# Spreading the later keys of a gated DeltaNet layer over more merge gates, and loading and pausing the triangular solve differently

## The chip, the core and the metric

The kernel runs on one core of a Trainium2 chip. The metric is device time in microseconds (us) of one execution. The engines are TensorE (PE, matmuls and transposes), VectorE (DVE), ScalarE (ACT), GpSimd (POOL) and SyncE (SP, which here issues every DMA). A difference of about 0.5% is what a measurement of this kernel can tell from no change.

## The reference, cut to what matters

One decoder layer on 512 tokens of width 2048, all in float32. After an adaptive norm, `h` is projected into many parts; a sliding-window attention and a gated DeltaNet run side by side, each goes through an output projection, and two sigmoid gates merge them.

```
proj = h @ w_in
aq, ak, av, ag, d_qkv, dz, db, da, mg_a, mg_b = jnp.split(proj, _split_points(), axis=-1)
...
d_qkv = causal_conv_silu(d_qkv, conv_w)
dq, dk, dv = jnp.split(d_qkv, [DN_KEY, 2 * DN_KEY], axis=-1)
...
L = jnp.where(strict, jnp.einsum('bhncd,bhnsd->bhncs', k_beta, k) * decay, 0.0)
t_inv = lax.linalg.triangular_solve(eye + L, jnp.broadcast_to(eye, L.shape),
                                    left_side=True, lower=True, unit_diagonal=True)
u = t_inv @ v_beta
w = t_inv @ (k_beta * jnp.exp(g)[..., None])
...
y = jax.nn.sigmoid(mg_a) * y_a + jax.nn.sigmoid(mg_b) * y_b
return x + gate * (y @ w_out)
```

There are 16 key heads and 32 value heads of width 128; `k` is normed per token, and `L` belongs to a chunk of 64 tokens. So the keys come first, then their chunk matrices `L`, then the inverse of `eye + L`, and only then can the heads (queries, values, scan) run. The merge gates `mg_a` and `mg_b` need only `h`.

## The kernel before

**Tiles.** Every projection is cut into channel tiles of 128 output channels by 512 tokens (`channel_tile`). A weight in float32 is split into a high and a low part (`split`: `whi` by ACT, `wlo` by DVE, two halves of 128x1024 each per tile), and each product is three matmuls (`mm3`, lines 237 to 239), so a tile is 48 matmuls of 128x512. After every two of its 16 steps `pump` is called: 8 pumps to a tile. All other work is written as generators that `pump` advances: `live` ones count pumps (a `yield 3` resumes three pumps later), `slow` ones get a budget per pump.

**Stages.** The start computes `h` and, in passing, the accumulators of four keys (`NST`). Then comes the stage of the keys (about 138 to 545 us of the profile): 31 tiles, namely 16 merge gates `mb`, the 12 keys 4 to 15, and 3 merge gates `ma`. The merge gates are there as PE work that asks little of others: a tanh by ACT and a store. Then 16 groups of heads of 5 tiles each, the output projections, the attention, and the end.

**A key** (`keys`, lines 648 to 692) takes about 19 pumps after its tile: convolution (ACT, then 3 DVE instructions and a silu), transposes by PE into the PSUM tile `ptk`, sums of squares by ACT (`sumsq`, four `junk`), three pumps later the norm by DVE (`rsqrt`, lines 55 to 65, and L658: a chain of eleven instructions on 128x4 elements, `ss`, `rky`, `rkt`), the scaling of `k` by ACT (L664), transposes back by PE into `ptkT` (L271), a product `pkk` by PE (L677) times the decay mask `E` (two tiles of 128x512 per key, loaded by DMA, masked by POOL in lines 710 and 711, exponentiated by ACT, multiplied by DVE in line 683), and stores of `lt_d`. `ptk`, `ptkT` and `pkk` take turns in two PSUM buffers of the tag `tp`; `E` has four buffers.

**The solve** (`solve`) inverts 64x64 triangles, 128 at once, by 124 DVE instructions (lines 754 and 761, `atmp` and `A`) for half 0 (heads 0 to 15, `s0`), and again for half 1 (`s1`). It is `slow` work: `s0` has a budget of 0.85 per pump, 1.2 from a late gate on; `s1` 0 until `s0` is done, then 1.1, and 0.6 among the heads. `solve_load` waits until the eight keys of its half have stored, loads `A` in two DMAs per 64 partitions, and lets `solve` start. `hold` is a number of pumps in which `slow` work is not advanced; in the stage of the keys (`keep_order` is true there) it has no effect.

**Order.** `mixed` sets the order of the tiles, and `plan` the order of the weight loads that follows from it: four `mb` ahead (`NFIRST`), keys 4 to 7 one after the other, then key and gate by turns (k8, mb4, k9, mb5, ... k15, mb11), then mb12 to mb15 and ma0 to ma2. The order on each engine is then set by a scheduler, which moves an instruction ahead where its buffers allow it; so DMAs and work for a later head can stand among those of an earlier one.

Of the kernel before, what the change touches and what calls it, by code (L numbers as in the profile page):

```python
# [19 lines left out]
KT = D // P  # L20
NTB = T // P
EPS = 1e-6
KH = 16
VH = 32
QH = 32
HD = 64
# [3 lines left out]
TWO_PI_LO = 3.0199159819567e-07  # L30
MAGIC = float(0x5F3759DF)
NST = 4
NFIRST = 4
STW = 320 + NST * P


class Layer:
# [43 lines left out]
    def pump(self):  # L81
        self.weight_tick()
        with self.behind() if self.keep_order else nullcontext():
            for e in list(self.live):
                e[1] -= 1
                if e[1] <= 0:
                    self.step(e)
        held, self.hold = self.hold > 0 and not self.keep_order, max(self.hold - 1, 0)
        with self.behind():
            for e in [] if held else list(self.slow):  # L90
                e[2] += e[1]
                while e in self.slow and e[2] >= e[3]:
                    e[2] -= e[3]
                    self.step_slow(e)
        for q in list(self.side.values()):
            if not q:
                continue
            q[0][2] += q[0][1]
            while q and q[0][2] >= 1.0:
                q[0][2] -= 1.0  # L100
                if next(q[0][0], True):
                    q.pop(0)
# [44 lines left out]

    def mixed(self):

        first = [("k", g) for g in range(NST, 8)]  # L150
        turns = [x for g in range(8, KH) for x in (("k", g), ("mb", g - 8 + NFIRST))]
        return first + turns + [("mb", j) for j in range(8 + NFIRST, KT)]


    def plan(self):
        a, jobs = self.a, []
        wi = lambda name, t: jobs.append((name, a["w_ch"][t]))
        jobs += [(f"st{u}", a["w_st"][u]) for u in range(KT // 2)]
        for j in range(NFIRST):
            wi(f"mb{j}", 96 + j)  # L160
# [408 lines left out]
    def conv(self, pool, ps, t, y):  # L569

        nc = self.nc
        w = self.convh[:, t, :]
        nc.scalar.activation(y, ps, AF.Copy, scale=w[:, 3:4])
        yield 1
        self.hold = max(self.hold, 1)
        for j, s in ((2, 1), (1, 2), (0, 3)):
            nc.vector.scalar_tensor_tensor(  # L577
                out=y[:, s:], in0=ps[:, : T - s], scalar=w[:, j : j + 1], in1=y[:, s:], op0=ALU.mult, op1=ALU.add
            )
        yield 2  # L580
        th = pool.tile([P, T], F32, tag="th", name="th")
        nc.scalar.activation(th, y, AF.Tanh)
        yield 1
        nc.vector.scalar_tensor_tensor(out=y, in0=th, scalar=1.0, in1=y, op0=ALU.add, op1=ALU.mult)


    def deltanet(self):
        tc, nc, a = self.tc, self.nc, self.a
        dram = self.dram
        self.lt_d = dram.tile([2, 2, 16, 4, HD, HD], F32, name="lt_d")  # L590
        self.lab_d = dram.tile([VH, HD, 4, HD], F32, name="lab_d")
        self.ta_d = dram.tile([2, 16, 4, HD, HD], F32, name="ta_d")
        self.ts_d = dram.tile([2, 2, 16, 4, HD, HD], F32, name="ts_d")
        self.kT_d = dram.tile([KH, P, T], F32, name="kT_d")
        self.k_d = dram.tile([KH, P, T], F32, name="k_d")
        self.o_d = dram.tile([VH, P, T], F32, name="o_d")
        with ExitStack() as ps:
            self.pmm = ps.enter_context(tc.tile_pool(name="pmm", bufs=2, space=PSUM, reuse_waits="tile"))
            self.ptp = ps.enter_context(tc.tile_pool(name="ptp", bufs=2, space=PSUM, reuse_waits="tile"))
            self.gwk = ps.enter_context(tc.tile_pool(name="gwk", bufs=1, reuse_waits="tile"))  # L600
            sol1 = ps.enter_context(tc.tile_pool(name="sol1", bufs=1, side="right", reuse_waits="tile"))
            with ExitStack() as sa:
                wk = sa.enter_context(tc.tile_pool(name="dnA", bufs=2, reuse_waits="tile"))
                sol0 = sa.enter_context(tc.tile_pool(name="sol0", bufs=1, reuse_waits="tile"))
                gp = sa.enter_context(tc.tile_pool(name="gates", bufs=1, reuse_waits="tile"))
                self.go(self.gates(gp), 1)
                self.keys_done, self.solve_in = [], {}
                self.keep_order = True
                for g in range(NST):
                    self.go(self.keys(wk, g, self.acc_k[g]), 10 + 8 * g)  # L610
                for j in range(NFIRST):
                    self.merge_gate("mb", j, self.mb_d)
                self.go(self.solve_load(sol0, 0), 1)
                self.go(self.solve_load(sol1, 1), 1)
                s0 = self.paced(self.solve(sol0, 0, nc.vector), 0.85)
                s1 = self.paced(self.solve(sol1, 1, nc.vector), 0.0)
                for kind, j in self.mixed():
                    if kind == "k":
                        self.go(self.keys(wk, j, self.channel_tile(f"k{j}")), 0)
                    else:  # L620
                        self.merge_gate("mb", j, self.mb_d)
                        if j == KT - 4:
                            s0[1] = 1.2
                for j in range(3):
                    self.merge_gate("ma", j, self.ma_d)
                    if s0 not in self.slow:
                        s1[1] = 1.1
                self.drain_live()
                self.drain_slow(s0)
                self.keep_order = False  # L630
                s1[1] = 0.6
            with ExitStack() as sb:
                wk = sb.enter_context(tc.tile_pool(name="dnB", bufs=2, reuse_waits="tile"))
                self.tt = []
                for n in range(4):
                    t = wk.tile([P, NTB, P], F32, tag=f"tt{n}", name=f"tt{n}", bufs=1)
                    nc.gpsimd.memset(t[HD:P, :, 0:HD], 0.0)
                    self.tt.append(t)
                for g in range(KH):
                    if g == 8:  # L640
                        self.drain_slow(s1)
                    self.heads(wk, g)
                for j in range(3, 5):
                    self.merge_gate("ma", j, self.ma_d)
                self.drain_live()
        self.dump("o", self.o_d)

    def keys(self, wk, g, ps):

        nc = self.nc  # L650
# [4 lines left out]
        self.transpose4(pt, lambda c: y[:, c * P : (c + 1) * P])  # L655
        ss = self.sumsq(wk, pt)
        yield 3
        nc.vector.tensor_scalar(out=ss, in0=ss, scalar1=EPS, scalar2=None, op0=ALU.add)  # L658
        rk = self.rsqrt(wk, ss, NTB, "rk")
        E = [self.decay_load(wk, 2 * g + e) for e in range(2)]  # L660
        yield 2
        k = wk.tile([P, NTB, P], F32, tag="k", name="k")
# [22 lines left out]
        for e in range(2):  # L685
            h = 2 * g + e
            b, hl = h // 16, h % 16
            for k2 in range(2):
                s = slice(k2 * HD, (k2 + 1) * HD)
# [24 lines left out]

    def solve_load(self, wk, b):
        nc = self.nc
        while not all(g in self.keys_done for g in range(8 * b, 8 * b + 8)):
            yield 1
        yield 3
        A = wk.tile([P, HD, HD], F32, tag=f"A{b}", name="A", bufs=1)  # L720
        bet = wk.tile([P, HD], F32, tag=f"bet{b}", name="bet", bufs=1)
        for k2 in range(2):
            s = slice(k2 * HD, (k2 + 1) * HD)
            nc.sync.dma_start(
                out=bet[s],
                in_=self.b_rows.rearrange("h (c k i) -> k (h c) i", c=4, k=2)[k2, b * HD : (b + 1) * HD, :],
            )
        for q in range(2):
            for k2 in range(2):
                s = slice(k2 * HD, (k2 + 1) * HD)  # L730
                r = slice(q * 32, (q + 1) * 32)
                nc.sync.dma_start(out=A[s, r], in_=self.lt_d[b, k2].rearrange("h c j i -> (h c) j i")[:, r])
            yield 4
        self.solve_in[b] = A, bet

    def solve(self, wk, b, eng):
# [828 lines left out]
```

## Time and profile before

| | us |
|---|---|
| median of 3 runs | 2956.26 (2944.69 to 2958.72) |
| the profiled execution | 2954.11 |
| its span | 2952.3 |
| PE busy in the span | 2879.0 (98%) |
| DVE busy in the span | 1794.3 (61%) |

Rows of groups and of the timeline name line, engine, operation and `out<-in` tile; a bracket at a row's end is the engine's idle time before it and what ended it. Rows of waits give the total, the number of times and the longest. Rows of windows give the stretch, its length, the busy time of PE, of PE's weight loads, of DVE, ACT and POOL with their instructions in brackets, the granted clock of PE as a share of full speed, the share of DMA, and GB/s. "Issue" of a DMA is on SP.

### The profile page before, as it was taken

What the parts mean: (1) busy time and instruction counts of PE and PEld (TensorE: products, weight loads), DVE (VectorE), ACT (ScalarE), POOL (GpSimd) and SP (SyncE); (2) the same over time, 40 slices, a digit from 0 to 9 for tenths busy, and PEclk for the clock granted to TensorE, in tenths of its full rate; (3) what the DMA queues carried; (4) which work ended last, traced back from release to release, by engine and by line L of the source; (5) the groups of instructions that cost most, each with busy time, mean ns of one, the idle gap of its engine ahead of it and who ended that gap; (6) DMA issues with size and microseconds to landing.
All of it is one profiled execution on the core that took longest, in us unless ns stands there. A gap on an engine that the chain in (4) does not pass through costs nothing.

```text
span 2952.3 us, 38088 instructions
## 1 busy us (share of the span) xinstructions
PE 2879.0 (98%) x14556; PEld 2358.8 (80%) x14556; DVE 1794.3 (61%) x2915; ACT 1085.7 (37%) x2113; POOL 232.7 (8%) x204
## 2 busy tenths in 40 slices
PE   8899999999999999999999999999999999999988
PEld 6678777788888888888888788888788788888867
DVE  6766998777775545555445453434755655553697
ACT  4345333333334333333333322312344444432333
POOL 0022220100000001100000000000100000000011
PEclk9999999999999999999999999999999999999999
DMA  9746545633335334333332675554322232375562
GB/s 380 282 155 206 173 136 168 185 121 110 123 108 154 123 118 134 112 126 115 121 111 98 219 268 179 196 163 157 106 88 88 76 102 102 106 269 169 180 200 85
DMA packets 175305, 451.12 MB, mean 153 GB/s; under 512 B 72434, under 2 KB 74994, under 8 KB 138898
## 3 DMA queue, kind: packets, MB, share of 16 engines
q1 hardware_dynamic: 175122, 448.70, 45.8%
q8 instruction: 114, 1.87, 0.3%
q14 instruction: 69, 0.56, 0.1%
HBM read 386.95 MB, written 59.45 MB: 151 GB/s over the span
## 4 chain that ended last, share of the span: by engine, by line
PE 84%; DVE 8%; DMA 2%; ACT 2%; issue 2%; POOL 1%; SPq 0%; POOLq 0%; DVEq 0%; ACTq 0%
PE mm L237 24%; PE mm L238 24%; PE mm L239 24%; DVE wlo L53 2%; DVE wa L411 2%; ACT whi L52 1%; PE S L1205 1%; PE pv L915 1%; PE po L934 1%; PE O L1256 1%; PE pP L271 1%; PE po L933 1%; PE pd L930 1%; PE pp L905 1%; DMA qe<-eg_rows 1%
## 5 line engine op out<-in xcount | busy, mean ns | idle before, releaser
L237 PE MATMUL mm<-hh,whi 128*128 128x512 f32 x2784 | 1132.8, 407 | 0.7 <-ACT mth L260 0.7
L239 PE MATMUL mm<-hh,wlo 128*128 128x512 f32 x2784 | 1092.4, 392 | 0.0
L238 PE MATMUL mm<-hl,whi 128*128 128x512 f32 x2784 | 1090.1, 392 | 0.0
L53 DVE TENSOR_TENSOR wlo<-raw,whi 128x1024 fp32r<-128x1024 f32 (+1 forms) x452 | 553.9, 1227 | 531.6 <-ACT whi L52 525.0
L52 ACT CAST whi<-raw 128x1024 fp32r<-128x1024 f32 (+1 forms) x452 | 470.8, 1043 | 1004.3 <-PE mm L238 949.7
L239 PEld LDWEIGHTS mm<-hh,wlo 128*128 128x128 f32 x2784 | 524.1, 188 | 112.8
L237 PEld LDWEIGHTS mm<-hh,whi 128*128 128x128 f32 x2784 | 525.5, 189 | 110.4 <-issue 8.4
L238 PEld LDWEIGHTS mm<-hl,whi 128*128 128x128 f32 x2784 | 525.9, 189 | 99.7 <-issue 0.8
L237 PE MATMUL mm<-oh,whi 128*128 128x512 f32 x512 | 200.4, 393 | 1.2 <-ACT whi L52 0.9
L238 PE MATMUL mm<-ol,whi 128*128 128x512 f32 x512 | 199.5, 390 | 0.5 <-DVE ol L53 0.5
L239 PE MATMUL mm<-oh,wlo 128*128 128x512 f32 x512 | 199.4, 390 | 0.5 <-DVE wlo L53 0.5
L862 POOL TENSOR_TENSOR qe<-qe,yq 128x512 f32<-128x512 f32 x32 | 50.1, 1585 | 923.9 <-DMA qe<-eg_rows 853.1
L237 PEld LDWEIGHTS mm<-oh,whi 128*128 128x128 f32 x512 | 96.1, 188 | 23.2 <-ACT whi L52 1.3
L238 PEld LDWEIGHTS mm<-ol,whi 128*128 128x128 f32 x512 | 96.1, 188 | 22.1 <-DVE ol L53 1.4
L710 POOL TENSOR_TENSOR E<-E,neg_g 128x512 f32<-128x512 f32 x64 | 75.7, 1183 | 478.3 <-DMA E<-g_rows 381.5
L239 PEld LDWEIGHTS mm<-oh,wlo 128*128 128x128 f32 x512 | 96.1, 188 | 20.9 <-DVE wlo L53 1.2
L761 DVE TENSOR_TENSOR A<-A,atmp 128x62 f32<-128x62 f32 (+30 forms) x124 | 108.8, 877 | 1.5
L754 DVE TENSOR_TENSOR atmp<-A 128x62 f32<-128x62 f32 (+30 forms) x124 | 108.4, 874 | 1.2
L908 DVE SCALAR_TENSOR_TENSOR r<-pp,neg_eg,vt 128x128 f32<-128x128 f32 x96 | 29.2, 346 | 77.9 <-PE pp L905 76.5
L1229 ACT ACTIVATE sm<-sm,mx,rs 128x256 f32<-128x256 f32 (+1 forms) x128 | 71.7, 562 | 3.3 <-DVE mx L1224 3.3
L577 DVE SCALAR_TENSOR_TENSOR yv<-mm,convh,yv 128x511 f32<-128x511 f32 (+2 forms) x96 | 71.4, 744 | 1.6
L238 PE MATMUL m<-wlo,hh 128*128 128x512 f32 x128 | 52.1, 407 | 9.9 <-DVE wlo L53 9.9
(331 smaller groups left out, 3161.9 us busy)
## 6 DMA issues: line engine op xcount, KB each, us to landing
raw<-in_w_ch SPq DMA_DIRECT2D x158, 1024.0 KB
wa<-in_w_ada_ss SPq DMA_DIRECT2D x32, 1024.0 KB
raw<-in_w_od SPq DMA_DIRECT2D x32, 1024.0 KB
E<-g_rows SPq DMA_DIRECT2D x64, 256.0 KB
gw<-in_w_ada_gate SPq DMA_DIRECT2D x16, 1024.0 KB
raw<-in_w_os SPq DMA_DIRECT2D x16, 1024.0 KB
qe<-eg_rows SPq DMA_DIRECT2D x32, 256.0 KB
o_d<-zh SPq DMA_DIRECT2D x32, 256.0 KB
```

Of the source, the lines that this page charges most:

```text
L52: self.nc.scalar.copy(out=hi, in_=src)
L53: self.nc.vector.tensor_tensor(out=lo, in0=src, in1=hi.bitcast(F32), op=ALU.subtract)
L237: nc.tensor.matmul(ps, lhsT=wh, rhs=xh, start=first, stop=False)
L238: nc.tensor.matmul(ps, lhsT=wh, rhs=xl, start=False, stop=False)
L239: self.last_mm = nc.tensor.matmul(ps, lhsT=wl, rhs=xh, start=False, stop=last).ins
L411: nc.vector.scalar_tensor_tensor(out=wa, in0=wa, scalar=1.0, in1=scb, op0=ALU.mult, op1=ALU.mult, accum_out=t[:, j : j + 1])
L577: nc.vector.scalar_tensor_tensor(out=y[:, s:], in0=ps[:, : T - s], scalar=w[:, j : j + 1], in1=y[:, s:], op0=ALU.mult, op1=ALU.add)
L710: nc.gpsimd.tensor_tensor(out=E, in0=E, in1=ng, op=ALU.add)
L754: eng.tensor_tensor(out=t, in0=A[:, m : m + 1, m + 1 :].to_broadcast([P, m, n]), in1=A[:, :m, m : m + 1].to_broadcast([P, m, n]), op=ALU.mult,
L761: eng.tensor_tensor(out=A[:, :m, m + 1 :], in0=A[:, :m, m + 1 :], in1=t, op=ALU.add)
L862: nc.gpsimd.tensor_tensor(out=qf, in0=qf, in1=q, op=ALU.mult)
L1229: nc.scalar.activation(t, t, AF.Exp, scale=r[:, h : h + 1], bias=mx[:, h : h + 1], accum_out=den[:, h : h + 1])
```

## The change

Five edits. (1) `NFIRST` is 3: one merge gate fewer ahead of key 4. (2) `mixed` puts one gate behind each even key from 8 on and two behind each odd one (k8, mb3, k9, mb4, mb5, k10, mb6, ...), so that the last key comes two tiles later, at position 24 of 31 instead of 22. (3) `keys` sets `hold` to 2 where its norm begins, and `hold` now acts in the stage of the keys too (the convolution no longer sets it there). (4) `solve_load` loads the 32 rows of the first four keys of a half as soon as those are stored, and the other 32 rows after the eighth; `solve` may start four pumps sooner behind the last key. (5) The budget of `s0` is 0.82 instead of 0.85 and rises to 1.2 one gate later (mb13).

```diff
-NFIRST = 4
+NFIRST = 3
...
-        held, self.hold = self.hold > 0 and not self.keep_order, max(self.hold - 1, 0)
+        held, self.hold = self.hold > 0, max(self.hold - 1, 0)
...
-        first = [("k", g) for g in range(NST, 8)]
-        turns = [x for g in range(8, KH) for x in (("k", g), ("mb", g - 8 + NFIRST))]
-        return first + turns + [("mb", j) for j in range(8 + NFIRST, KT)]
+        order = [("k", g) for g in range(NST, 8)]
+        mb = iter(range(NFIRST, KT))
+        for g in range(8, KH):
+            order.append(("k", g))
+            order += [("mb", next(mb)) for _ in range(1 + g % 2)]
+        return order + [("mb", j) for j in mb]
...
-        self.hold = max(self.hold, 1)
+        self.hold = max(self.hold, 0 if self.keep_order else 1)
...
-                s0 = self.paced(self.solve(sol0, 0, nc.vector), 0.85)
+                s0 = self.paced(self.solve(sol0, 0, nc.vector), 0.82)
...
-                        if j == KT - 4:
+                        if j == KT - 3:
                             s0[1] = 1.2
...
         ss = self.sumsq(wk, pt)
         yield 3
+        self.hold = 2
...
-        while not all(g in self.keys_done for g in range(8 * b, 8 * b + 8)):
-            yield 1
-        yield 3
...
         for q in range(2):
+            while not all(g in self.keys_done for g in range(8 * b + 4 * q, 8 * b + 4 * q + 4)):
+                yield 1
+            yield 3
             for k2 in range(2):
-                s = slice(k2 * HD, (k2 + 1) * HD)
-                r = slice(q * 32, (q + 1) * 32)
-                nc.sync.dma_start(out=A[s, r], in_=self.lt_d[b, k2].rearrange("h c j i -> (h c) j i")[:, r])
-            yield 4
+                r = slice(32 * q, 32 * q + 32)
+                s = slice(k2 * HD + 32 * q, k2 * HD + 32 * q + 32)
...
+                nc.sync.dma_start(out=A[s], in_=self.lt_d[b, k2].rearrange("h c j i -> (h c) j i")[r])
+        yield 4
         self.solve_in[b] = A, bet
```

What this does to the order is shown at three places. Numbers behind a name tell buffers' contents apart. Every engine runs the same instructions as before, but for `A<-lt_d`, which is 8 DMAs of 32x4096 instead of 8 of 64x2048.

**The norm of a late key on DVE.** Before, key 14: `ss`, `rky`, `rkt` are the norm, `atmp` and `A` the solve, `wlo` a half of a weight.

```order
L658 TENSOR_SCALAR ss<-ss 128x4
L754 TENSOR_TENSOR atmp<-A 128x972
L59 TENSOR_SCALAR rky<-ss 128x4
L62 SCALAR_TENSOR_TENSOR rkt<-rky 128x4
L63 TENSOR_TENSOR rkt<-rkt,ss 128x4
L64 SCALAR_TENSOR_TENSOR rky<-rkt,rky 128x4
L62 SCALAR_TENSOR_TENSOR rkt<-rky 128x4
L761 TENSOR_TENSOR A<-A,atmp 128x36x27
L63 TENSOR_TENSOR rkt<-rkt,ss 128x4
L53 TENSOR_TENSOR wlo<-raw,whi 128x1024
L64 SCALAR_TENSOR_TENSOR rky<-rkt,rky 128x4
L754 TENSOR_TENSOR atmp<-A 128x962
```

Now, the norm of the same key.

```order
L662 TENSOR_SCALAR ss<-ss 128x4
L59 TENSOR_SCALAR rky<-ss 128x4
L62 SCALAR_TENSOR_TENSOR rkt<-rky 128x4
L63 TENSOR_TENSOR rkt<-rkt,ss 128x4
L64 SCALAR_TENSOR_TENSOR rky<-rkt,rky 128x4
L62 SCALAR_TENSOR_TENSOR rkt<-rky 128x4
L63 TENSOR_TENSOR rkt<-rkt,ss 128x4
L64 SCALAR_TENSOR_TENSOR rky<-rkt,rky 128x4
L62 SCALAR_TENSOR_TENSOR rkt<-rky 128x4
L63 TENSOR_TENSOR rkt<-rkt,ss 128x4
L64 SCALAR_TENSOR_TENSOR rky<-rkt,rky 128x4
L757 TENSOR_TENSOR atmp<-A 128x902
```

The eleven instructions stand together now, with no instruction of the solve among them; so it is for keys 9 to 14, while the chain of key 15 still has two. On PE, `ptkT` of each key from 9 on now stands at one tile behind its `ptk` (0.94 to 1.0 tiles); before it stood up to 1.37 tiles behind, at key 13, and 1.22 at key 10.

**The start of the heads on ACT.** Before: `yv` is the convolution of value tile 0, `th_4846` its tanh, `ptv` PE's transposes of it; `E_5286` and `E_5288` are the decay masks of the second group of heads, five tiles ahead of their use.

```order
L573 ACTIVATE yv_4792<-mm_4686,convh_127 128x512
L856 ACTIVATE E_5286<-E_5286 128x512
L856 ACTIVATE E_5288<-E_5288 128x512
L52 CAST whi_4908<-raw_4707 128x1024
L582 ACTIVATE th_4846<-yv_4792 128x512
L812 COPY vt_4885<-ptv_4880 128x512
```

Now, the same value tile: `E_4715` is a mask of the first group, `E_5274` one of the second.

```order
L576 ACTIVATE yv_4772<-mm_4658,convh_127 128x512
L702 ACTIVATE junk_4745,ss_4742<-ptq_4737 128x128
L52 CAST whi_4836<-raw_4677 128x1024
L702 ACTIVATE junk_4747,ss_4742<-ptq_4737 128x128
L859 ACTIVATE E_4715<-E_4715 128x512
L702 ACTIVATE junk_4749,ss_4742<-ptq_4737 128x128
L585 ACTIVATE th_4826<-yv_4772 128x512
L52 CAST whi_4892<-raw_4677 128x1024
L815 COPY vt_4867<-ptv_4862 128x512
L52 CAST whi_4956<-raw_4782 128x1024
L576 ACTIVATE yv_4896<-mm_4761,convh_127 128x512
L859 ACTIVATE E_5274<-E_5274 128x512
```

The masks of the second group now stand behind the tanh and the transposes of value tile 0. The masks of the first group, which stood ahead of `yq`, now stand between `yq` and that tanh.

**Keys 3 and 4 on DVE.** Before, the norm of key 3 stands alone behind the products of key 2 with their masks.

```order
L683 TENSOR_TENSOR E<-pkk,E 128x512 x2
L658 TENSOR_SCALAR ss<-ss 128x4
L59 TENSOR_SCALAR rky<-ss 128x4
L62 SCALAR_TENSOR_TENSOR rkt<-rky 128x4
L63 TENSOR_TENSOR rkt<-rkt,ss 128x4
L64 SCALAR_TENSOR_TENSOR rky<-rkt,rky 128x4
```

Now, a part of the norms of key 4 and key 3, which run together; `x2` is one instruction for each of the two keys.

```order
L662 TENSOR_SCALAR ss<-ss 128x4
L64 SCALAR_TENSOR_TENSOR rky<-rkt,rky 128x4
L59 TENSOR_SCALAR rky<-ss 128x4
L62 SCALAR_TENSOR_TENSOR rkt<-rky 128x4 x2
L63 TENSOR_TENSOR rkt<-rkt,ss 128x4 x2
L64 SCALAR_TENSOR_TENSOR rky<-rkt,rky 128x4 x2
```

With three gates ahead, key 4 ends its tile two pumps before key 3 may begin. PE's `ptk` of key 3 stands 0.31 tiles behind that of key 4, where the two were 0.84 apart.

More of the change, by code (lines that the diff above doesn't have):

```diff
@@ L716, in solve_load @@
         nc = self.nc
-        while not all(g in self.keys_done for g in range(8 * b, 8 * b + 8)):
-            yield 1
-        yield 3
         A = wk.tile([P, HD, HD], F32, tag=f"A{b}", name="A", bufs=1)
         bet = wk.tile([P, HD], F32, tag=f"bet{b}", name="bet", bufs=1)
-        for k2 in range(2):
-            s = slice(k2 * HD, (k2 + 1) * HD)
[L724 to L727, printed above, removed]
         for q in range(2):
+            while not all(g in self.keys_done for g in range(8 * b + 4 * q, 8 * b + 4 * q + 4)):
+                yield 1
+            yield 3
             for k2 in range(2):
-                s = slice(k2 * HD, (k2 + 1) * HD)
-                r = slice(q * 32, (q + 1) * 32)
-                nc.sync.dma_start(out=A[s, r], in_=self.lt_d[b, k2].rearrange("h c j i -> (h c) j i")[:, r])
-            yield 4
+                r = slice(32 * q, 32 * q + 32)
+                s = slice(k2 * HD + 32 * q, k2 * HD + 32 * q + 32)
+                if q == 0:
+                    nc.sync.dma_start(
+                        out=bet[k2 * HD : (k2 + 1) * HD],
+                        in_=self.b_rows.rearrange("h (c k i) -> k (h c) i", c=4, k=2)[k2, b * HD : (b + 1) * HD, :],
+                    )
+                nc.sync.dma_start(out=A[s], in_=self.lt_d[b, k2].rearrange("h c j i -> (h c) j i")[r])
+        yield 4
         self.solve_in[b] = A, bet
```

## The prediction

> **What bounds the kernel.** First the page.
>
> ```profile
> span 2952.3 us, 38088 instructions
> PE 2879.0 (98%) x14556; PEld 2358.8 (80%) x14556; DVE 1794.3 (61%) x2915; ACT 1085.7 (37%) x2113; POOL 232.7 (8%) x204
> PE   8899999999999999999999999999999999999988
> DVE  6766998777775545555445453434755655553697
> ```
>
> PE has work in 98% of the span, and the change takes no matmul away. So it can only win idle time of PE and lost clock, and only where it moves instructions. The digits of DVE show where another engine comes near PE: slices 5 and 6, in the stage of the keys. The windows over the stages, in the order first keys, keys beside the solve, last gates, first eight groups of heads:
>
> ```profile
> 138.00:300.00 162.00, 157.14 (x761) 128.81 (x762) 104.35 (x204) 79.59 (x196) 36.56 (x36) 0.99 0.59 183
> 300.00:480.00 180.00, 166.63 (x758) 136.22 (x757) 163.51 (x236) 67.19 (x152) 37.15 (x32) 0.97 0.46 151
> 480.00:545.00 65.00, 65.00 (x289) 53.81 (x288) 49.65 (x69) 23.99 (x26) 0.00 (x0) 1.00 0.70 203
> 545.00:1040.00 495.00, 488.29 (x2556) 405.56 (x2555) 335.76 (x550) 188.92 (x406) 50.81 (x46) 1.00 0.41 126
> ```
>
> Between 300 and 480 us DVE is busy for 163.5 of 180 us, PE idles for 13.4 and the granted clock is 0.97. The window without idle time gives a tile: 65.00 us / 289 matmuls x 48 = 10.8 us. Who PE waits for, in the windows 150 to 300, 300 to 480 and 540 to 1040:
>
> ```profile
> PE ptkT L271 <- ACT k L664: 4.7, 6, 1.5
> ...
> PE ptkT L271 <- ACT k L664: 13.4, 6, 2.9
> ...
> PE ptv L271 <- DVE yv L584: 6.7, 3, 5.3
> ```
>
> All of the idle time between 300 and 480 is one wait, for the scaled `k`. In the heads it is 6.7 us, of which 5.3 is one wait at their start. And the waits cost clock, by windows of 20 us:
>
> ```profile
> 410.00:430.00 20.00, 18.08 (x81) 14.87 (x81) 18.30 (x24) 6.33 (x13) 5.08 (x4) 0.91 0.32 108
> 430.00:450.00 20.00, 17.13 (x75) 13.85 (x74) 16.64 (x24) 8.29 (x20) 5.22 (x4) 0.91 0.48 171
> 470.00:490.00 20.00, 18.71 (x81) 15.51 (x82) 16.87 (x21) 6.92 (x12) 0.78 (x4) 0.91 0.57 182
> 570.00:590.00 20.00, 14.67 (x89) 11.60 (x88) 12.42 (x17) 6.20 (x9) 4.16 (x4) 0.91 0.39 106
> ```
>
> Each of the four lost 0.09 x 20 = 1.8 us to the clock, three beside the solve (5.4) and one at the start of the heads (1.8).
>
> **What the wait for k is made of.** The norm of key 14 on DVE, and PE behind it:
>
> ```profile
> 434.70 0.16 DVE L658 TENSOR_SCALAR ss<-ss 128x4 f32<-128x4 f32 x1
> 434.82 1.17 DVE L754 TENSOR_TENSOR atmp<-A 128x972 f32<-128x972 f32 x1
> ...
> 437.51 1.61 DVE L761 TENSOR_TENSOR A<-A,atmp 128x972 f32<-128x972 f32 x1
> 439.05 1.00 DVE L63 TENSOR_TENSOR rkt<-rkt,ss 128x4 f32<-128x4 f32 x1
> 439.97 1.21 DVE L53 TENSOR_TENSOR wlo<-raw,whi 128x1024 fp32r<-128x1024 f32 x1
> ...
> 441.62 1.15 DVE L754 TENSOR_TENSOR atmp<-A 128x962 f32<-128x962 f32 x1
> ...
> 443.07 0.16 DVE L64 SCALAR_TENSOR_TENSOR rky<-rkt,rky 128x4 f32<-128x4 f32 x1
> ...
> 443.69 0.33 PE L271 MATMUL ptkT<-ident,k 128*128 128x128 f32 x1 [2.87 <-ACT k L664]
> ```
>
> The chain takes 443.23 - 434.70 = 8.5 us; 1.17 + 1.61 + 1.15 = 3.9 of it are the solve's. Without those it ends 3.9 us sooner, which is more than PE waits here, 2.87, the longest.
>
> **The change part by part.**
>
> *The pause* (`hold`, two of eight pumps). It takes the solve out of the chains of keys 9 to 14, some 3.9 us each by key 14; in key 15 two of its instructions stay. Nothing is dropped: the solve runs outside the chains, so DVE must have room. Per key and pair of tiles it now has 2 x 2 `wlo`, the key's own instructions and 16 pumps of solve:
>
> ```profile
> L754 DVE TENSOR_TENSOR atmp<-A 128x810 f32<-128x810 f32 (+30 forms) x45 | 43.8, 973 | 0.2
> L53 DVE TENSOR_TENSOR wlo<-raw,whi 128x1024 fp32r<-128x1024 f32 x27 | 33.5, 1242 | 12.6 <-ACT whi L52 12.5
> L577 DVE SCALAR_TENSOR_TENSOR y<-mm,convh,y 128x511 f32<-128x511 f32 (+2 forms) x18 | 13.3, 740 | 0.0
> L683 DVE TENSOR_TENSOR E<-pkk,E 128x512 f32<-128x512 f32 x14 | 9.1, 684 | 2.8 <-PE pkk L677 2.0 <-issue 0.8
> ```
>
> *The spread* gives that room. A key costs DVE 3 x 0.74 + 2 x 0.68 + a silu and a norm, some 6.5 us (estimate); a tile costs 2 x 1.24 = 2.5. Before, 2 tiles hold one key: 5.0 + 6.5 + 16 x 0.85 of solve (a unit of its budget is about one us, by 0.97 an instruction) = 25.1 us, against 2 x 10.8 and some 4 of small matmuls for PE: level. Now 24 pumps go with the odd keys and 16 with the even, on average 20: 6.2 + 6.5 + 18 x 0.82 (two paused) = 27.5, against 27 + 4 = 31. So DVE no longer lags, and a burst is made up within a tile. What works against it is the order: `ptkT` stands nearer behind its `ptk`, by 0.43 tiles (4.6 us) at key 13 and 0.22 (2.4) at key 10. The early keys, whose chains hold no solve, still wait for 4.7 us among eight, 0.6 each; by that row 7 x 0.6 = 4.1 would be left, and none if the pause does all. I take 3.0. Sum: -13.4 - 5.4 + 3.0 = **-15.8 us** (from -18.8 to 0).
>
> The Trainium skill ("TensorE: Matmul & The Clock Gate", section "What's actually happening") has the clock halved after an idle window of about 3.4 us; by that only the wait of 5.3 us would cost clock, and the sum would be 5.4 us less of a gain. The trace shows 0.91 behind waits of 1.9 to 2.9 us too, so the measured loss is used.
>
> *The start of the heads.* The chain that makes the 5.3 us:
>
> ```profile
> 544.93 0.88 SPq L703 DMA_DIRECT2D E<-g_rows  x2
> ...
> 564.43 0.91 SPq L703 DMA_DIRECT2D E<-g_rows  x2
> 570.23 1.39 POOL L710 TENSOR_TENSOR E<-E,neg_g 128x512 f32<-128x512 f32 x1 [5.06 <-DMA E<-g_rows]
> 572.85 0.63 ACT L856 ACTIVATE E<-E 128x512 f32<-128x512 f32 x1 [7.82 <-POOL E L711]
> 576.04 0.62 ACT L582 ACTIVATE th<-yv 128x512 f32<-128x512 f32 x1
> 578.14 1.09 PE L271 MATMUL ptv<-ident,yv 128*128 128x128 f32 x4 [5.33 <-DVE yv L584]
> ```
>
> ACT sat 7.82 us before a mask that the next group of heads needs; the tanh of the value tile stood behind it. In the new order that mask stands behind the tanh and `ptv`. What stands ahead of the tanh now is a mask of the first group, issued about a tile before (544.9 us in the old trace; now behind one weight load more, some 550), so at POOL by about 556 and done 4 us later, ahead of the tanh at 570. **-5.3 - 1.8 = -7.1 us** (from -7.1 to 0).
>
> *Three gates ahead.* Keys 3 and 4 now come together, on two PSUM buffers. DVE runs both chains in one stretch, and PE's product of key 2 must wait for the buffer that `k` of key 4 gives free. The nearest row is the early wait, at most 1.5 us; I take two of these, **+3.0 us** (from 0 to the whole of a chain at four places, see the third rival). SP is passed in this stretch by the first load of `A`, which waits for the stores of key 3, ahead of a weight load that has about two tiles of slack; that is taken at nothing.
>
> *Load in two parts, budget, end of the solve.* The bytes are the same. The solve of half 0 may start about 1.4 tiles sooner and ends about 0.9 later (29.25 to 30.1 of 31 tiles, counted in pumps), since it is paused; its stores are read 1.9 tiles later at the earliest. Half 1 starts later, by about 25 us (estimate: a tile, and the eight pumps at 1.1). Before:
>
> ```profile
> 942.43 12.22 SPq L781 DMA_DIRECT2D ts_d<-A  x4
> ...
> 1035.30 1.91 SPq L847 DMA_DIRECT2D tt<-ts_d  x3
> ```
>
> It was stored 80 us ahead of its first reader, so 55 are left. At nothing, both.
>
> Sum: -15.8 - 7.1 + 3.0 = -19.9. Against the profiled execution, 2954.1 us, that is 2934.2. The median of the runs lies 2.2 above that execution, so the forecast for the median is **2936 us**.
>
> **Rivals.** *First, the late waits stay.* What stretches the norm may be POOL as much as the solve: an instruction on 128x4 takes 1.00 in key 14's chain where its like takes 0.16, while POOL masks.
>
> ```profile
> L710 POOL TENSOR_TENSOR E<-E,neg_g 128x512 f32<-128x512 f32 x14 | 19.1, 1368 | 146.4 <-DMA E<-g_rows 104.8 <-DVE rkt L62 41.6
> L711 POOL TENSOR_SCALAR_AFFINE_SELECT E<-E 128x512 f32<-128x512 f32 x14 | 17.1, 1225 | 1.0
> ```
>
> The masks of a key take 2 x (1.37 + 1.23) = 5.2 us; if all of that fell on the chain, it would eat the 3.9 won, and `ptkT` stands nearer. Then the wait is as long as before: -7.1 + 3.0 = -4.1, 2952 for the median. For it: the 1.00. Against it: those slow rows are in the 8.5 us already. The Trainium skill ("GPSIMD Engine Reference", section "1. Specifications") says that POOL shares its interfaces to SBUF with VectorE; the 1.00 agrees. Chance 0.12.
>
> *Second, the start of the heads keeps its wait*, on a mask of the first group, if its load lands behind the stores of the solve, which now come just ahead of it: -15.8 + 3.0 = -12.8, 2943.5. Chance 0.20.
>
> *Third, slower: the early keys pile up.* If at four places (the product of key 2, `ptkT` of keys 4, 3 and 5) PE waits for a whole chain of the kind that key 3 had, from 215.41 to 221.32 us, with a dip of the clock each, that is 4 x (5.9 + 1.8) = 30.8 more.
>
> ```profile
> 215.41 0.16 DVE L658 TENSOR_SCALAR ss<-ss 128x4 f32<-128x4 f32 x1
> ...
> 221.16 0.16 DVE L64 SCALAR_TENSOR_TENSOR rky<-rkt,rky 128x4 f32<-128x4 f32 x1
> ```
>
> -22.9 + 30.8 = +7.9, 2964. It decides from 22.9 us of new waits on. Against it: a transpose follows its norm by one tile, and DVE is busy for 104 of 162 us there. Chance 0.08.
>
> **Numbers.** The forecast has 0.55, the rivals 0.12, 0.20 and 0.08, and 0.05 is left for what I don't see. Low end: every wait gone and no early loss, -25.9, 2928 in the profiled execution's terms; runs of the kernel before spread down to 2944.7, 9 under it, so 2922. High end: 2956, with the first two rivals inside and the third left out. 0.5% (about what a measurement can tell here) is 14.8 us: under 2941.5 lies the forecast but for 0.05, 0.06 of the second rival and 0.02 of the rest, 0.58; slower is 0.08; 0.34 is within.
>
> **What would show it.** Right: the wait of `ptkT` for `k` between 300 and 500 us falls from 13.4 to about 3; the windows there show a clock of 1.00; no `ptv` wait of over 1 us near 575; early `ptkT` and `pkk` waits of 6 to 9 us in all instead of 4.7; norms of 4 to 6 us. Wrong: late waits of over 8 us (first rival), ACT idle for POOL by the tanh of the first value tile (second), early waits of over 15 us (third), or idle time of PE in a place not named here.

## The result, and the profile after

The changed kernel takes 2934.87 us (median of 6 runs, 2930.44 to 2937.08) against 2956.88 us for the kernel before (6 runs, 2944.69 to 2958.79): ratio 0.9929, 95% interval 0.9911 to 0.9948. That is 22.0 us less, faster by more than 0.5%. The profiled execution took 2931.54 us, 22.6 less than the one of before. The windows over the stages of the changed kernel come first (columns as before: PE, PE's weight loads, DVE, ACT and POOL, then clock, share of DMA and GB/s), and behind them three windows of 20 us at places where the kernel before lost clock.

```profile
138.00:300.00 162.00, 155.90 (x754) 126.49 (x753) 101.36 (x219) 80.10 (x205) 35.06 (x36) 0.99 0.62 189
300.00:480.00 180.00, 178.12 (x830) 146.90 (x829) 164.93 (x226) 69.55 (x144) 38.21 (x31) 1.00 0.51 159
545.00:1040.00 495.00, 493.06 (x2615) 409.29 (x2616) 348.67 (x578) 193.45 (x421) 57.90 (x52) 1.00 0.41 129
410.00:430.00 20.00, 20.00 (x95) 16.68 (x94) 18.19 (x26) 8.08 (x17) 5.96 (x4) 1.00 0.64 200
430.00:450.00 20.00, 20.00 (x91) 16.53 (x90) 17.40 (x26) 6.23 (x14) 0.73 (x1) 1.00 0.47 148
560.00:580.00 20.00, 20.00 (x121) 16.19 (x120) 16.56 (x26) 7.51 (x13) 4.56 (x4) 1.00 0.50 146
```

Beside the solve PE idles for 1.9 us instead of 13.4, among the heads for 1.9 instead of 6.7, and the clock is whole in both. DVE is as busy as before between 300 and 480 us (164.9 of 180, before 163.5). So the stage was not won by giving DVE less to do. Whom PE waits for now, in the windows 138 to 300, 300 to 500 and 540 to 1040 us:

```profile
PE ptkT L274 <- ACT k L668: 3.5, 3, 1.7
PE mm L240 <- ACT whi L52: 1.3, 1, 1.3
PE ptk L274 <- DVE E L687: 0.6, 1, 0.6
PE mm L242 <- DVE wlo L53: 0.5, 1, 0.5
...
PE ptkT L274 <- ACT k L668: 0.9, 1, 0.9
PE mm L242 <- DVE wlo L53: 0.8, 1, 0.8
PE mm L240 <- ACT whi L52: 0.2, 1, 0.2
...
PE ptv L274 <- DVE yv L587: 1.9, 3, 0.9
```

The norm of key 14 on DVE, whose chain took 8.5 us before, and POOL's first mask in it:

```profile
447.62 0.16 DVE L662 TENSOR_SCALAR ss<-ss 128x4 f32<-128x4 f32 x1
447.81 0.17 DVE L59 TENSOR_SCALAR rky<-ss 128x4 int32<-128x4 int32 x1
...
449.39 0.94 DVE L63 TENSOR_TENSOR rkt<-rkt,ss 128x4 f32<-128x4 f32 x1
450.37 0.16 DVE L64 SCALAR_TENSOR_TENSOR rky<-rkt,rky 128x4 f32<-128x4 f32 x1
450.45 1.54 DVE L757 TENSOR_TENSOR atmp<-A 128x902 f32<-128x902 f32 x1
```

```profile
449.27 1.05 POOL L714 TENSOR_TENSOR E<-E,neg_g 128x512 f32<-128x512 f32 x1 [26.50 <-DVE rky L64]
```

It takes 450.53 - 447.62 = 2.9 us, and those of keys 10 to 13 take 2.1 each. One row alone is slow (0.94), and it begins 0.12 us after POOL's mask. Nine of the other ten had begun before POOL did. So the pause took out two things: the solve's instructions, and with them the masks, which had stretched the chain because it lasted into them. Key 15, whose chain still holds two instructions of the solve, takes 6.9 us, with two slow rows, and the one late wait for `k` (0.9) is behind it.

At the start of the heads, on ACT: the second mask of the first group, then `yv`'s tanh, which now waits 1.52 us for DVE and not for POOL.

```profile
549.56 0.63 ACT L859 ACTIVATE E<-E 128x512 f32<-128x512 f32 x1
...
551.98 0.63 ACT L585 ACTIVATE th<-yv 128x512 f32<-128x512 f32 x1 [1.52 <-DVE yv L580]
```

### The profile page after: what moved, and what is told of

Its sections match the earlier page's. It is cut to its first block, busy times and chain, and to the rows that moved or that the text cites. A ratio compares the mean times of both kernels' runs of the same rounds, so it can differ in the third digit from the quotient of the medians.

```text
span 2929.7 us, 38073 instructions
## 1 busy us (share of the span) xinstructions
PE 2870.6 (98%) x14556; PEld 2351.2 (80%) x14556; DVE 1787.2 (61%) x2915; ACT 1085.1 (37%) x2113; POOL 243.0 (8%) x204
## 4 chain that ended last, share of the span: by engine, by line
PE 84%; DVE 3%; DMA 2%; issue 1%; ACT 1%; POOL 1%; SPq 0%; POOLq 0%; DVEq 0%; ACTq 0%
PE mm L240 24%; PE mm L242 24%; PE mm L241 24%; DVE wlo L53 1%; PE S L1208 1%; PE pv L918 1%; PE po L937 1%; PE O L1259 1%; PE pP L274 1%; PE po L936 1%; PE pd L933 1%; PE pp L908 1%; PE m L241 1%; PE m L242 1%; PE m L240 1%
## 5 line engine op out<-in xcount | busy, mean ns | idle before, releaser
L240 PE MATMUL mm<-hh,whi 128*128 128x512 f32 x2784 | 1130.7, 406 | 2.3 <-ACT whi L52 1.6
L240 PEld LDWEIGHTS mm<-hh,whi 128*128 128x128 f32 x2784 | 523.7, 188 | 112.3 <-issue 8.4
L240 PE MATMUL mm<-oh,whi 128*128 128x512 f32 x512 | 200.6, 393 | 2.6 <-ACT oh L52 1.7
L240 PEld LDWEIGHTS mm<-oh,whi 128*128 128x128 f32 x512 | 96.0, 188 | 24.8 <-ACT oh L52 3.0
L580 DVE SCALAR_TENSOR_TENSOR yv<-mm,convh,yv 128x511 f32<-128x511 f32 (+2 forms) x96 | 71.5, 745 | 1.6
```

Source lines behind the costliest of these rows:

```text
L240: nc.tensor.matmul(ps, lhsT=wh, rhs=xh, start=first, stop=False)
L580: nc.vector.scalar_tensor_tensor(out=y[:, s:], in0=ps[:, : T - s], scalar=w[:, j : j + 1], in1=y[:, s:], op0=ALU.mult, op1=ALU.add)
```

## The experiments

Theory A was that the pause takes the late waits away; theory B, that the spread does, by leaving DVE room. Each kernel's ratio is against runs of the kernel before on the same chip. Diffs show the core of the edit.

**The pause alone.** The kernel before, with this:

```diff
-        held, self.hold = self.hold > 0 and not self.keep_order, max(self.hold - 1, 0)
+        held, self.hold = self.hold > 0, max(self.hold - 1, 0)
...
-        self.hold = max(self.hold, 1)
+        self.hold = max(self.hold, 0 if self.keep_order else 1)
...
         ss = self.sumsq(wk, pt)
         yield 3
+        self.hold = 2
```

> The kernel before with the pause alone (hold of two pumps at the norm of a key, as in the change); four gates ahead, one gate behind each key, the old load and the old budget stay. Theory A, the pause alone takes the late waits away, the spread only gives room that is not needed: ptkT waits for k between 300 and 500 us fall from 13.4 us to under 3, clock 1.00 there, no ptv wait over 1 us near 575 (its order has the masks of the second group behind the tanh too), no new early waits; about 2935 us, ratio 0.993. Theory B, the spread is what does it: with one gate per key DVE is level with PE, so solve work that is paused comes back as waits of PE for wlo or for k, 6 to 13 us of them stay, and only the start of the heads is won (7.1 us); 2945 to 2950 us, ratio 0.996 to 0.998.

Measured: 2931.24 us, ratio 0.9925 (0.9913 to 0.9938): as much as the whole change. The window from 300 to 480 us, and PE's only wait for `k` between 300 and 520:

```profile
300.00:480.00 180.00, 177.04 (x830) 146.40 (x829) 168.25 (x240) 70.55 (x152) 42.81 (x32) 1.00 0.54 169
```

```profile
PE ptkT L271 <- ACT k L665: 2.4, 1, 2.4
```

The one wait left for `k` is that of key 10, whose chain still has solve in it. DVE is busy for 168.25 of 180 us, more than in either kernel, and PE idles for 3.0 of the 180 in all. Theory A holds; the spread is not needed for the room. The start of the heads is won by the pause alone too (waits of 3.6 us, none above 1.3): the masks of the second group stand behind the tanh here as well. By what steps the scheduler comes from the pause to that order was not followed.

**The change without the pause.** The changed kernel, less one line:

```diff
-        self.hold = 2
```

> The changed kernel without the pause (the one line that sets hold to 2 in the norm is left out), all else as changed. Theory A: the solve is back in the chains of keys 9 to 15, each some 3 to 4 us longer, and PE waits for k some 2 us at four to six of them with the clock loss behind it: 8 to 18 us in all, 2943 to 2953 us, ratio 0.9955 to 0.999. Theory B: DVE has room between the keys, the late waits stay under 3 us, 2935 us, ratio 0.993. The masks of the second group of heads: one of them stands ahead of the tanh of value tile 0, fewer than before, so a ptv wait of 0 to 2 us.

Measured: 2957.14 us, ratio 1.0011 (1.0002 to 1.0019). The whole gain is gone. PE's waits between 300 and 520 us, then between 520 and 1040:

```profile
PE ptkT L274 <- ACT k L667: 14.0, 6, 2.9
PE mm L242 <- DVE wlo L53: 0.5, 1, 0.5
PE mm L240 <- ACT whi L52: 0.2, 1, 0.2
...
PE ptv L274 <- DVE yv L587: 3.7, 5, 1.2
PE mm L242 <- DVE wlo L53: 2.8, 1, 2.8
```

The six late waits are back in full, somewhat above the range that theory A gave. The start of the heads has no `ptv` wait above 1.2 us, but one for `wlo` of 2.8 in its place: 6.5 us in all, before 6.7. Where the last 3 us over the kernel before come from was not followed.

**The spread alone.** The kernel before with the new `mixed` (four gates ahead, so its list starts at gate 4), and the budget's raise behind key 15:

```diff
-        first = [("k", g) for g in range(NST, 8)]
-        turns = [x for g in range(8, KH) for x in (("k", g), ("mb", g - 8 + NFIRST))]
-        return first + turns + [("mb", j) for j in range(8 + NFIRST, KT)]
+        order = [("k", g) for g in range(NST, 8)]
+        mb = iter(range(NFIRST, KT))
+        for g in range(8, KH):
+            order.append(("k", g))
+            order += [("mb", next(mb)) for _ in range(1 + g % 2)]
+        return order + [("mb", j) for j in mb]
...
-                        if j == KT - 4:
+                        if j == KT - 2:
```

> The kernel before with the spread of the later keys alone (one gate behind each even key, two behind each odd one; four gates ahead, no pause, old load, budget 0.85, its raise behind key 15). Theory A, the spread brings nothing to the chains: solve and masks stay in them, the late waits stay at 11 to 15 us; as the start of the heads keeps only one of the two masks of the second group ahead of the transposes, up to 5 us may go there; ratio 0.997 to 1.001. Theory B, room on DVE lets the solve run outside the chains: late waits under 5 us, ratio 0.993 to 0.995.

Measured: 2952.11 us, ratio 0.9984 (0.9973 to 0.9995). PE's waits, 300 to 520 us and 520 to 1040:

```profile
PE ptkT L274 <- ACT k L667: 10.6, 5, 2.8
...
PE mm L240 <- DVE yq L580: 5.5, 1, 5.5
PE ptv L274 <- DVE yv L587: 1.3, 2, 0.7
```

The chains of keys 10 to 15 take 6.0 to 10.5 us, and 10.6 of 13.4 us of waiting stay. At the start of the heads one wait of 5.3 us has given way to another of 5.5: the solve of half 1, a tile later now, stands ahead of the convolution of the first query tile, and DVE waits there for its load.

```profile
DVE A L749 <- DMA A<-lt_d: 4.0, 1, 4.0
```

**Four gates ahead, the rest as changed.**

```diff
-NFIRST = 3
+NFIRST = 4
...
-                        if j == KT - 3:
+                        if j == KT - 2:
```

> The changed kernel with four gates ahead of the keys again (spread, pause, load and budget as changed; the raise of the budget one gate later, so that it still falls behind key 15). Theory: keys 3 and 4 no longer come together, the early waits of ptk for E (0.6) and the ones for whi and wlo near 266 us go, but four waits for k of 0.2 to 0.8 us come back; late waits stay under 3 us: between 2 us faster and 2 us slower than the changed kernel, 2933 to 2937 us, ratio 0.993. Rival: three gates ahead is what gained, since a key that starts one tile sooner frees DVE later: 5 us or more slower than the changed kernel, ratio 0.995 or above.

Measured: 2935.62 us, ratio 0.9938 (0.9925 to 0.9952), no different from the changed kernel within the intervals. Behind that stand two opposite effects in the profiled execution: PE's early waits are 3.3 us instead of 5.9, and at 547 us a wait for `yq` is there as in the spread alone (`PE mm L240 <- DVE yq L580`), with a clock of 0.83 from 540 to 560 us.

```profile
PE ptkT L274 <- ACT k L668: 3.3, 4, 1.2
...
PE mm L240 <- DVE yq L580: 5.5, 1, 5.5
```

The load of half 1 is not what PE waits for here: it was issued at 497.8 us, and DVE has no wait for it. On ACT the first step of that convolution stands behind a `whi` that waits 4.38 us for PE, and starts at 542.4 us; in the changed kernel it starts at 536.9. So with the spread, three gates ahead cost 2.6 us more of early waits (5.9 instead of 3.3), and four cost 6.0 more at the start of the heads (7.9 instead of 1.9). The times of the two kernels are too near each other to show that difference.

**The old load, the rest as changed.**

```diff
-            while not all(g in self.keys_done for g in range(8 * b + 4 * q, 8 * b + 4 * q + 4)):
+        while not all(g in self.keys_done for g in range(8 * b, 8 * b + 8)):
...
-                nc.sync.dma_start(out=A[s], in_=self.lt_d[b, k2].rearrange("h c j i -> (h c) j i")[r])
+                nc.sync.dma_start(out=A[s, r], in_=self.lt_d[b, k2].rearrange("h c j i -> (h c) j i")[:, r])
```

> The changed kernel with the old load of the solve (A loaded by two column halves after all eight keys, start four pumps later). Theory: nobody waits for the solve's start, so nothing changes: 2935 us, ratio 0.993, and the solve of half 0 ends about a tile later (some 11 us). Rival: the earlier start is what leaves DVE time by the last keys; without it the solve still runs when the heads begin and PE waits for wlo or yv there: 5 us or more slower, ratio 0.995 or above.

Measured: 2930.97 us, ratio 0.9924 (0.9911 to 0.9936): the load in two parts is worth nothing. The solve of half 0 did not end later either (its stores start at 526.0 us, in the changed kernel at 527.1), other than expected. The early waits are of another kind: 6.4 us for `k` and none for `whi` or `wlo`, where the changed kernel has 3.5 and 1.8.

**POOL's masks out of the chain, no pause.** The next question is what in the chain made it long: the solve's instructions, or POOL's masks beside it (theories D and C). The kernel before, with loads and masks of keys 9 to 15 ahead of the key's convolution; DVE, ACT and PE keep their order around the norm.

```diff
+        early = g >= 9
+        E = [self.decay_load(wk, 2 * g + e) for e in range(2 if early else 0)]
+        for e in range(len(E)):
+            self.decay_mask(E[e], 2 * g + e)
         y = wk.tile([P, T], F32, tag="y", name="y", bufs=3)
...
-        E = [self.decay_load(wk, 2 * g + e) for e in range(2)]
+        E = E or [self.decay_load(wk, 2 * g + e) for e in range(2)]
...
-        for e in range(2):
+        for e in range(0 if early else 2):
             self.decay_mask(E[e], 2 * g + e)
```

> The kernel before (no pause), with the loads of E and POOL's masks of keys 9 to 15 a tile or more earlier, ahead of the key's convolution; the order on DVE, ACT and PE around the norm is that of before, with the solve in the chain. Theory C, POOL stretches the chain: the rows of about 1.0 us on 128x4 elements in the norm fall to 0.16 to 0.47, the late chains of 8.5 to 12.4 us lose 2 to 2.5 us each, and since PE's late waits are at most 2.9 us, 8 to 12 of the 13.4 us go, and the clock loss with them: ratio 0.995 to 0.997. Theory D, the solve's long instructions themselves are what makes those rows slow and the chain long: rows and waits stay, ratio 0.999 to 1.001.

Measured: 2938.30 us, ratio 0.9951 (0.9938 to 0.9963), 15.6 us less, with the solve still in every late chain. The groups of the norm's three repeated lines between 320 and 480 us (busy time and mean ns), in the kernel before:

```profile
L64 DVE SCALAR_TENSOR_TENSOR rky<-rkt,rky 128x4 f32<-128x4 f32 x18 | 7.8, 434 | 0.3
L63 DVE TENSOR_TENSOR rkt<-rkt,ss 128x4 f32<-128x4 f32 x18 | 7.0, 389 | 0.3
L62 DVE SCALAR_TENSOR_TENSOR rkt<-rky 128x4 f32<-128x4 f32 x18 | 6.6, 368 | 0.2
```

and with the masks away:

```profile
L64 DVE SCALAR_TENSOR_TENSOR rky<-rkt,rky 128x4 f32<-128x4 f32 x18 | 2.9, 160 | 0.3
L63 DVE TENSOR_TENSOR rkt<-rkt,ss 128x4 f32<-128x4 f32 x18 | 2.9, 159 | 0.3
L62 DVE SCALAR_TENSOR_TENSOR rkt<-rky 128x4 f32<-128x4 f32 x18 | 2.8, 158 | 0.2
```

That is 21.4 - 8.6 = 12.8 us over six chains, 2.1 each; no row of the norm is above 0.17 us. PE's waits between 300 and 520 us fall to this:

```profile
PE ptk L271 <- DVE y L584: 1.9, 3, 1.0
PE ptkT L271 <- ACT k L668: 1.1, 2, 0.7
```

So theory C: POOL's masks stretch the chain, and 2 to 3 us of it were enough to decide, since PE's waits were 1.9 to 2.9. The start of the heads keeps its wait here (5.2 us), as nothing there was changed.

**The pause, with the masks pushed into the chain.** The pause alone, with the loads of `E` ahead of the norm's wait and the masks at its start, for all keys:

```diff
         ss = self.sumsq(wk, pt)
+        E = [self.decay_load(wk, 2 * g + e) for e in range(2)]
         yield 3
         self.hold = 2
+        for e in range(2):
+            self.decay_mask(E[e], 2 * g + e)
...
-        E = [self.decay_load(wk, 2 * g + e) for e in range(2)]
...
-        for e in range(2):
-            self.decay_mask(E[e], 2 * g + e)
```

> The pause alone (as in the run with the pause only), but the loads of E are issued ahead of the norm's wait and POOL's masks are emitted at the start of the norm, so that they fall into the chain, which in the run with the pause only they come too late for. Theory C: the late chains grow from 2.1 to 4 to 5 us by two or three rows of 1.0 us, and PE does not wait for them, since only what ends after the tile behind them matters: late waits under 4 us, ratio 0.992 to 0.994. Rival: a chain of 4 to 5 us already makes PE wait some 1 to 2 us per key: ratio 0.995 to 0.997. Theory D: the chains stay at 2.1 us.

Measured: 2926.05 us, ratio 0.9910 (0.9895 to 0.9925). The norm of key 15, and POOL beside it:

```profile
444.51 1.04 DVE L662 TENSOR_SCALAR ss<-ss 128x4 f32<-128x4 f32 x1
445.58 0.97 DVE L59 TENSOR_SCALAR rky<-ss 128x4 int32<-128x4 int32 x1
446.59 0.55 DVE L62 SCALAR_TENSOR_TENSOR rkt<-rky 128x4 f32<-128x4 f32 x1
...
448.94 0.16 DVE L64 SCALAR_TENSOR_TENSOR rky<-rkt,rky 128x4 f32<-128x4 f32 x1
```

```profile
440.53 6.00 POOL L711 TENSOR_TENSOR E<-E,neg_g 128x512 f32<-128x512 f32 x2 [18.20 <-DMA E<-g_rows]
446.49 1.22 POOL L712 TENSOR_SCALAR_AFFINE_SELECT E<-E 128x512 f32<-128x512 f32 x2
```

The chain is 4.6 us with masks and without solve. PE waits for `k` in one place beside the solve:

```profile
331.13 0.33 PE L271 MATMUL ptkT<-ident,k 128*128 128x128 f32 x1 [1.65 <-ACT k L667]
```

That is behind key 10, whose chain (323.92 to 330.68 us) still has instructions of the solve in it. Behind keys 11 to 15, whose chains hold the masks alone, PE does not wait for `k` at all. Together with the run before: with the solve alone in the chain (6 to 9 us) PE waits 1.1 us for `k`, with the masks alone (3 to 5 us) not at all, with both 13.4. The masks of the early keys are done sooner too, and PE's waits between 138 and 300 us are 2.5 us instead of 4.4 in the run with the pause alone.

**The start of the heads alone.** The kernel before, with the exponentials of the second group of heads kept behind the matmuls issued by then:

```diff
-        for e in range(2):
-            nc.scalar.activation(M[e], M[e], AF.Exp)
+        with self.behind() if g == 1 else nullcontext():
+            for e in range(2):
+                nc.scalar.activation(M[e], M[e], AF.Exp)
```

> The kernel before, and only the exponentials of the masks of the second group of heads are kept behind the matmuls that the program has issued by then, so that on ACT they stand behind the tanh of the first two value tiles. The stage of the keys is as before. Theory: the ptv wait of 5.3 us near 578 us goes and the clock loss of 1.8 us with it, the late waits of 13.4 us stay: 7 us less, ratio 0.9976 (0.996 to 0.9985). Rival: the wait moves to the next reader of those masks: ratio 0.999 to 1.001.

Measured: 2946.64 us, ratio 0.9981 (0.9972 to 0.9990), 7.3 us less. PE's waits, 300 to 520 us and 520 to 1040:

```profile
PE ptkT L271 <- ACT k L664: 13.9, 6, 3.0
...
PE ptv L271 <- DVE yv L584: 2.3, 3, 1.0
```

The wait of 5.3 us is gone and comes back nowhere. The masks away (15.6) and the start of the heads (7.3) add up to 22.9 us, about what the pause alone gives (22.3).

**One pump of pause instead of two.**

```diff
-        self.hold = 2
+        self.hold = 1
```

> The pause alone, with one pump instead of two. A pump is about 1.35 us, a bare chain 2.1 us. If what matters is the bare length, one pump lets one or two instructions of the solve (about 1 us each) and, by that, the first masks into the chain: chains of 4 to 6 us, late waits of 3 to 6 us, ratio 0.993 to 0.996. If the first pump alone matters (the norm is issued in it, ahead of the next pump's solve): chains of 2.1 us as with two pumps, ratio 0.992 to 0.993.

Measured: 2937.20 us, ratio 0.9951 (0.9938 to 0.9964). The chains of keys 10 to 15 are 2.1 to 10.3 us, and PE waits for four of the later keys:

```profile
PE ptkT L271 <- ACT k L665: 6.1, 4, 2.5
```

So the length of the pause matters, and two pumps (2 x 10.8 / 8 = 2.7 us) just cover the bare chain of 2.1 us.

**The pause, and the late masks a tile ahead.** The pause with the masks at the start of the norm for the early keys, and for keys 9 to 15 ahead of the convolution:

```diff
+        early = g >= 9
+        E = [self.decay_load(wk, 2 * g + e) for e in range(2 if early else 0)]
+        for e in range(len(E)):
+            self.decay_mask(E[e], 2 * g + e)
...
+        E = E or [self.decay_load(wk, 2 * g + e) for e in range(2)]
         yield 3
         self.hold = 2
+        for e in range(0 if early else 2):
+            self.decay_mask(E[e], 2 * g + e)
```

> The pause with POOL's masks of keys 9 to 15 a tile or more ahead of the norm, and those of keys 0 to 8 at the start of the norm as in the run with masks in the chain. All late chains become 2.1 us, key 9's about 4 to 6. If anything is still to be had from the late chains, it is what is left of late waits in the run with the masks in the chain, 1.7 us: ratio 0.990 to 0.992. If the chains are short enough already: the same 0.991 as that run.

Measured: 2926.42 us, ratio 0.9907 (0.9893 to 0.9922): the same as with the masks in the chain. With all late chains at 2.1 us but that of key 10, nothing more is to be had there: the waits for `k` fall to 0.3 us, and 2.8 us for `y` (`ptk` behind the convolution) stand in their place.

**The change, with the masks at the start of the norm.** The changed kernel with the diff of the run with masks in the chain.

> The changed kernel with the loads of E ahead of the norm's wait and POOL's masks at the start of the norm, for all keys. With the pause alone this gave 5 us (the first keys ended their chains sooner and PE waited 2 us less there). If that comes from the early masks themselves, the changed kernel gains as much: ratio 0.990 to 0.992; if it hangs on the order of the keys 3 and 4, it gains nothing: 0.993.

Measured: 2927.89 us, ratio 0.9909 (0.9896 to 0.9922). So the early masks add to the change as they do to the pause, 0.0020 and 0.0015 of the ratio, whatever the order of keys 3 and 4. Each of these steps is no wider than the intervals, but the three kernels with early masks lie at 0.9907 to 0.9910 and the three like them without at 0.9924 to 0.9929. They are the fastest versions found. The change's other edits add nothing to the pause here either (0.9909 against 0.9910).

## Why the prediction was right, and where its steps were not

The forecast was 2936 us, and 2934.87 came out; for the profiled execution 2934.2 against 2931.54. That the number is so near is in part luck: 5.4 us of the sum depend on which execution was profiled (see the end).

*Late keys, -15.8:* measured -13.4 + 1.9 - 5.4 = -16.9, by waits and clock of the two profiles. (With the two terms below, -16.9 - 6.6 + 0.8 = -22.7; the profiled execution lost 22.6.) The mechanism, the pause, was right, and the run without it shows that nothing else in the change does this. But two of its steps failed. "*The spread* gives that room": none was needed. The pause alone gives the whole gain, with DVE busy for 168.25 of 180 us, and the spread alone leaves 10.6 us of late waits. The level of DVE's load was worked out for a limit that did not bind; what bound was the length of one chain in the 10 us ahead of `ptkT`, made by the order inside DVE's queue and by POOL's masks together. And the chain was forecast at 4 to 6 us and came out at 2.1 for most keys: the working took out 3.9 us of solve and left the slow rows in. They went too, as the chain was over before POOL began (key 14: but for one row).

*The first rival* (0.12) named that second cause, POOL, and was right that it stretched the chain by 2 us and more. It was wrong that the masks stay when the solve goes; the run with the masks pushed in shows that PE would not have waited for `k` even so.

*The start of the heads, -7.1:* in the profiles -4.8 of waits and -1.8 of clock, -6.6; done by itself it was -7.3. The order shown ahead of the prediction was its cause, and the second rival (0.20), that a mask of the first group comes late, did not come about: that mask's exponential was through 1.8 us ahead of the tanh, which waited for DVE.

*Early keys, +3.0:* the term of the sum that was too large. Waits between 138 and 300 us went from 5.1 us (4.7 for `k`, 0.4 for `hl`) to 5.9, +0.8. The bunched keys cost 0.6 us by a buffer (`ptk` for `E`), while the waits for `k` fell from 4.7 to 3.5. The other 1.8, by `whi` and `wlo` at 266 us, are not the bunched keys' alone: the run with the old load bunches them as well and has none. Nor has the run with four gates and the new load. They come where three gates meet the first load of `A`, which stands ahead of a weight load on SP (issued at 243.1 us, with the old load at 237.9) and was taken at nothing; how that moves `whi` on ACT was not followed. With the old load the early waits are 7.0 us, so the sum is no worse for it. The third rival needed 22.9.

*Nothing for the load, the budget, the end of the solve:* the old load gives the same time. Half 0, forecast 0.9 tiles later, is stored from 527.1 us on, before from 527.2. Half 1, forecast 25 us later, has its last store issued at 972.8 us instead of 953.2 (19.6 later), with nobody waiting. What three gates ahead are for, the prediction did not see: with the spread and four gates ahead, PE waits 5.5 us for the first query tile at the start of the heads.

*The range:* its low end does not follow from its own terms, as 2928 less 9 is 2919 and not 2922. The result lies inside with either.

## What to carry to other kernels

Ahead of a transfer that another engine waits for, look at a short chain's span and not its busy time: eleven instructions of 0.16 us took 8.5 us because long, patient work stood between them in the same queue and another engine's work beside them. A pause of that work over the length of the bare chain cost nothing here, though the engine was 93% busy. When several edits come together, run the one line that touches the chain by itself.

## What the hardware showed

**POOL beside DVE.** While POOL masks tiles of 128x512, a DVE instruction on 128x4 elements takes up to 1.0 us instead of 0.16. This is shown by moving the masks alone (mean 434 to 160 ns). The traces show more: the slow row ends when POOL's instruction ends. In key 14's chain before:

```profile
436.31 1.07 POOL L710 TENSOR_TENSOR E<-E,neg_g 128x512 f32<-128x512 f32 x1 [20.64 <-DVE rkt L62]
436.50 0.90 DVE L64 SCALAR_TENSOR_TENSOR rky<-rkt,rky 128x4 f32<-128x4 f32 x1
438.07 1.96 POOL L710 TENSOR_TENSOR E<-E,neg_g 128x512 f32<-128x512 f32 x1
```

The first pair ends at 437.38 and 437.40 us; the second mask ends at 440.03, and the row of 1.00 us that the prediction shows at 439.05 ends at 440.05. So it is for all 42 slow rows of the norm (over 0.3 us) between 150 and 500 us of the kernel before, within 0.06 us. The row looks held up, then, and not slowed: its cost is what is left of POOL's instruction when it begins. Instructions with one input were hit as well (1.04 and 0.97 us in the run with masks in the chain). The Trainium skill ("GPSIMD Engine Reference", section "1. Specifications") says that POOL shares its SBUF interfaces with VectorE, with contention for DVE instructions in a 2-port mode or with two SBUF inputs. The slow rows with two inputs agree; whether those with one input ran in such a mode, no run here shows.

**The clock.** Behind waits of the same length the clock sometimes dips and sometimes doesn't. The kernel before lost three times 1.8 us in the stage of the keys. The run with the start of the heads alone has the same stage and the same six waits (13.9 us, up to 3.0), and lost clock once, 0.03 x 20 + 0.06 x 20 = 1.8 us:

```profile
320.00:340.00 20.00, 17.85 (x81) 14.26 (x80) 19.91 (x33) 6.45 (x18) 5.33 (x4) 0.97 0.50 165
340.00:360.00 20.00, 20.00 (x92) 16.70 (x91) 18.25 (x27) 7.36 (x17) 1.96 (x2) 0.94 0.43 138
...
440.00:460.00 20.00, 17.14 (x83) 14.35 (x84) 18.75 (x24) 8.82 (x21) 1.92 (x2) 1.00 0.39 123
```

So 5.4 us of the prediction's sum was a draw of that one execution; three dips or one would move it by 3.6 us. Lost clock is no accident of it, though: the mean granted clock was 0.991 to 0.994 in 15 executions of the kernel before, and 0.995 to 0.996 in the 5 of the pause alone. The Trainium skill ("TensorE: Matmul & The Clock Gate", section "What's actually happening") has a free-running window of about 3.4 us, which agrees with dips that come and go between executions; its rule of an idle window does not fit as it stands, since all these waits are shorter than 3.4 us. What decides it was not tried.
